# Rotary turn of the query and key heads: head by head on 32 partitions, or packed through DRAM onto 128 partitions

## The chip, the cores and the metric

The kernel runs on one core of a Trainium2 chip. TensorE (PE) multiplies, VectorE (DVE), ScalarE (ACT) and GpSimd (POOL) work element by element, SyncE (SP) issues most of the loads. The metric is the device time of one execution in microseconds (us), the median of several runs; lower is better.

## The reference

The kernel computes one decoder block for 512 tokens of width 1024. What concerns the change is the partial rotary embedding: of each of the 8 query heads and 2 key heads (width 128) the first 32 features are turned, 16 against 16; the other 96 stay as they are.

```python
def partial_rope(x, pos, rot_dim):          # rot_dim = 32 for q and k
    inv_freq = ROPE_THETA ** (-jnp.arange(0, rot_dim, 2, dtype=jnp.float32) / rot_dim)
    ang = pos.astype(jnp.float32)[..., None] * inv_freq
    ...
    xr = x[..., :rot_dim].astype(jnp.float32)
    x1, x2 = xr[..., : rot_dim // 2], xr[..., rot_dim // 2:]
    rot = jnp.concatenate([x1 * cos - x2 * sin, x2 * cos + x1 * sin], axis=-1)
    return jnp.concatenate([rot.astype(x.dtype), x[..., rot_dim:]], axis=-1)

# in the layer
q = partial_rope(q.reshape(bsz, s, N_HEADS, HEAD_DIM), positions, ROT_DIM)
k = partial_rope(k.reshape(bsz, s, N_KV_HEADS, HEAD_DIM), positions, ROT_DIM)
...
ki = layer_norm(ki, idx_k_ln_g, idx_k_ln_b)   # the indexer's key: normed, then turned by its own table
y_b = dsa_attention(q, k, v, qi, ki, wi)
```

## The kernel before, in words

**Layout.** Queries and keys are held transposed: features on the 128 partitions, the 512 tokens along a row. `qf[g]` holds heads 2g and 2g+1, `kf` the two key heads; each is `[128, 2, 512]` f32. The rows to be turned are partitions 0 to 31 of each.

**Every product is three.** Each f32 operand is split into a high part `hi` (ACT, a copy) and a rest `lo` (DVE, or POOL where the plan says so, a subtraction), and `mm3` (lines 107 to 109) issues hi by hi, hi by lo, lo by hi. Weights come in chunks: SP loads `raw`, ACT makes `hi` (line 163), DVE or POOL makes `lo` (line 167). `get(i, ahead=2)` prepares the chunk two further on before the current one is multiplied; there are three buffers each of `raw`, `hi` and `lo`.

**Order.** The schedule is written by hand: each engine executes its instructions in the order in which the code emits them, and waits by semaphores for the others. After the first projection (the key heads and query heads 0 to 3, until about 49 us) come eleven steps, counted by `qstep`: steps 0 and 1, then 2 and 3, are the two chunks each of `W_Q[0]` and `W_Q[1]` (the indexer's queries `qif`); 4, 5, 6 the three chunks of `vki` (values, the indexer's key, head weights); 7 and 8 `W_Q[2]`; 9 and 10 `W_Q[3]` (heads 4 to 7). At the start of step s `q_tasks` emits the list `QT[s]`, and only behind it the split of the chunk two further on. Then come eight chunks `W_AV` (the list `VT`).

**The key of the indexer.** In step 7 `ki_stats` takes mean and variance (DVE), and `rstd` on POOL (lines 430 and 431) makes the factor; `ki_norm` scales by it into `kin` on DVE (line 717). In the middle of step 8 `ki_T` has PE turn `kin` over (line 732, tile `kiT`), ACT and DVE bring it through `ki_a` and `ki_b`, and behind step 9 PE multiplies the result with the queries (lines 758 and 759, tile `idx`).

**POOL** has one queue: what it computes and the DMAs that it issues (`P.dma_start`) stand in one row, and a DMA that must wait for another to land holds up all behind it. In this stretch it issues the DMAs that lay out the tables `tab["q"]` and `tab["i"]` (lines 472 and 475), and then has little to do until `rstd`.

**The turn before.** For one head of 32 partitions `rope_a` shuffles the halves into `sh` (line 647), multiplies by the sine and by the cosine (648, 649), and `rope_b` adds (654): four DVE instructions, for ten heads, emitted in steps 0, 1, 2, 10 and with `W_AV`. `k_b` then splits the turned keys (`k_hi` on ACT, `k_lo` on DVE, line 435) in steps 7 and 8.

Of the kernel before, what the change touches and what calls it, by code (L numbers as in the profile page):

```python
# [9 lines left out]
F32 = mybir.dt.float32  # L10
# [48 lines left out]
def block_kernel(ctx: ExitStack, tc: tile.TileContext, x, x_t, w_in,  # L59
# [408 lines left out]
    def table_dma(kind, b):  # L468
        o = slice(b * 128, (b + 1) * 128)
        for h in range(2):  # L470
            if kind == "q":
                P.dma_start(tab["q"][h * 16:(h + 1) * 16, :, o], sn[b * 32:b * 32 + 16, 2 * h:2 * h + 2, :])
            else:
                for q in range(2):
                    P.dma_start(tab["i"][q * 64 + h * 8:q * 64 + h * 8 + 8, :, o],
                                sn[b * 32:b * 32 + 16:2, 2 * h:2 * h + 2, :])

    def run_chain(n):
        for _ in range(n):
# [116 lines left out]
    for kt in range(8):  # L596
        hi, lo = chunk[W1[kt]]
        V.tensor_sub(hT[kt][1], hfs[kt], f(hT[kt][0]))
        ensure(W1M[FIRST[kt]])
        if kt < 7:  # L600
            ensure(W1[kt + 1])
        wl = [(hi[:, 0, m * 128:(m + 1) * 128], lo[:, 0, m * 128:(m + 1) * 128]) for m in range(6)]
        hh, hl = hT[kt]
        kw = dict(skip_group_check=True)
        for m in range(6):
            T.matmul(outs[m], wl[m][0], hh, start=kt == 0, stop=False, **kw)
        for m in range(6):
            T.matmul(outs[m], wl[m][1], hh, start=False, stop=False, **kw)
        for m in range(6):
            T.matmul(outs[m], wl[m][0], hl, start=False, stop=kt == 7, **kw)  # L610
        if kt < 7:
            if kt < 5:
                low_w1(kt + 1)
            else:
                stream[W1[kt + 1]]["do"]()
            for k in (kt + 2,) if 0 < kt < 4 else (6, 7) if kt == 4 else ():
                row_scale(k)
            run_chain(kt == 1)
            ensure(W1M[BEHIND[kt]])
            stage_E(kt + 1)  # L620
        else:
            ensure(W_Q[0][1])
        if kt in (1, 2):
            A.activation(csb[:, (kt - 1) * 512:kt * 512], pc[:, (kt - 1) * 512:kt * 512], AF.Copy)
        if kt == 3:
            sines()
        if kt == 4:
            triu = mid.tile([128, 2, 128], F32, name="triu", tag="ql", bufs=2)[:, 0]
            SY.dma_start(triu, consts)
            for b in range(4):  # L630
                table_dma("q", b)
            for b in range(1, 4):
                table_dma("i", b)
            table_dma("i", 0)
    early.close()
    two.append(ctx.enter_context(tc.tile_pool(name="two", bufs=1, space=bass.MemoryType.PSUM)))
    for k in (6, 7):
        bank(k, "home")


    SW16 = [(p + 16) % 32 for p in range(32)]
    SW8 = [(p + 8) % 16 if p < 16 else p for p in range(32)]
    rp = {}

    def rope_a(key, v, kind, m, t0=0):
        sh = t512("sh")[:m, t0:]
        V.stream_shuffle(sh, v, SW16 if kind == "q" else SW8)
        V.tensor_mul(sh, sh, tab[kind][:m, 1, t0:])
        V.tensor_mul(v, v, tab[kind][:m, 0, t0:])
        rp[key] = (v, sh)  # L650
# [1 line left out]
    def rope_b(key):  # L652
        v, sh = rp[key]
        V.tensor_add(v, v, sh)


    kf = mid.tile([128, 2, S], F32, name="kf", tag="A0", bufs=1)
    qif = [mid.tile([128, 2, S], F32, name=f"qif{i}", tag=f"G{i}", bufs=1) for i in range(2)]
# [5 lines left out]
        A.activation(qf[m // 2][:, m % 2], pq[m], AF.Copy)  # L664
    for e in range(2):
        A.activation(kf[:, e], pk[e], AF.Copy)


    def qi_a(m):
# [14 lines left out]
    k_lo = mid.tile([128, 2, S], F32R, name="k_lo", tag="k_lo", bufs=1)  # L684

    k_pl = mid.tile([128, 2, 128], F32, name="k_pl")

    def k_a(h):
        rope_a(("k", h), kf[:32, h], "q", 32)

    def k_b(h):
        split(k_hi[:, h], k_lo[:, h], kf[:, h])
# [155 lines left out]
            iu[0] += 1  # L848
            n -= 1

    def q_rope(m):
        rope_a(("q", m), qf[m // 2][:32, m % 2], "q", 32)

    qstep = [0, 0]
    QT = {0: [lambda: q_rope(0), lambda: k_a(0)],
          1: [lambda: k_a(1), lambda: rope_b(("q", 0)), lambda: rope_b(("k", 0))],
          2: [lambda: rope_b(("k", 1)), lambda: qi_a(0)],
          3: [lambda: qi_b(0, 1), lambda: qi_a(1), lambda: qi_b(0, 0)],
          4: [lambda: qi_b(1, 1), lambda: qi_a(2), lambda: qi_b(1, 0)],
          5: [lambda: qi_b(2, 1), lambda: qi_a(3), lambda: qi_b(2, 0)],  # L860
          6: [lambda: qi_b(3, 1), lambda: qi_b(3, 0)],
          7: [ki_stats, lambda: k_b(0), ki_norm],
          8: [lambda: k_b(1)],
          10: [lambda: q_rope(1)]}

    def q_tasks():
        s = qstep[0]
# [39 lines left out]
        opt_b(W_Q[g], 8, hT, ((6, 7), (0, 1), (0, 1), (2, 3))[g], q_evac(g), q_tasks, q_post, q_mid, t0=0 if g > 1 else 128)  # L907


    vg = [mid.tile([128, 2, D], F32, name=f"vg{i}", tag=f"P{i}", bufs=1) for i in range(2)]  # L910
    lng = mid.tile([128, D], F32, name="lng", tag="G0", bufs=1)
    lnb = mid.tile([128, D], F32, name="lnb", tag="G1", bufs=1)
# [11 lines left out]
    def ws_mask():  # L924
        late["wmT"] = mid.tile([128, 8, 128], F32, name="wmT", tag="G2", bufs=1)
        V.tensor_tensor(late["wmT"], ws, triu[:, None, :].to_broadcast([128, 8, 128]), op=OP.mult)

    VT = {0: [lambda: q_rope(2), lambda: rope_b(("q", 1))],
          1: [lambda: q_rope(3), lambda: rope_b(("q", 2))],
          2: [lambda: q_rope(4), lambda: rope_b(("q", 3))],  # L930
          3: [lambda: q_rope(5), lambda: rope_b(("q", 4))],
          4: [lambda: q_rope(6), lambda: rope_b(("q", 5))],
          5: [lambda: q_rope(7), lambda: rope_b(("q", 6))],
          6: [lambda: rope_b(("q", 7)), load_bs], 7: [ws_mask]}
    for _ in range(16):
        bg.append((1.4, topk_max))
        bg.append((1.4, topk_replace))
# [1147 lines left out]
```

## Time and profile before

| | before |
|---|---|
| median of 3 runs | 784.74 us (784.25 to 785.29) |
| span of the profiled execution, first to last instruction | 783.3 us |
| mean granted TensorE clock | 0.993 |
| busy share PE, DVE, ACT, POOL | 99%, 85%, 55%, 23% |
| POOL's DMA queue (software dynamic) | 9232 packets, 30.15 MB, 15.2% of 16 engines' span |

The profiled execution's own time is its span and what lies around it; the median of the runs is 1.4 us above the span. An instruction's duration can overlap the next one on its engine, on PE above all: there the distance from start to start counts. A row of the timeline gives start, duration, engine, line, what is written from what, and in brackets how long the engine was idle before and what ended that.

### The profile page before, as it was taken

The page shows a single profiled execution, that of the slowest core. Times are in us where ns is not written, and L with a number is a line of the kernel's source. Part 1 is how long each engine was busy: PE and PEld are TensorE (multiplying, and loading weights), DVE is VectorE, ACT ScalarE, POOL GpSimd, SP SyncE. Part 2 cuts the span into 40 slices and gives each one's busy share as a digit, 9 for nine tenths or more (in the row PEclk, how much of TensorE's full clock was granted, in tenths as well). Part 3 has the DMA queues.
Part 4 walks back from the last instruction along what each step waited for, and adds up shares of the span by engine and source line. Part 5 has one row for each costly group of instructions (what it writes and reads, how often), then busy time and mean ns, then how long its engine had stood idle before and what let it go on. Part 6 is the DMA issues. An engine that isn't in the chain of part 4 may idle for free.

```text
span 783.3 us, 12307 instructions
## 1 busy us (share of the span) xinstructions
PE 774.1 (99%) x4579; PEld 688.5 (88%) x4579; DVE 666.6 (85%) x1128; ACT 427.3 (55%) x757; POOL 179.0 (23%) x234
## 2 busy tenths in 40 slices
PE   8999999999999999999999999999999999999996
PEld 7899888888888888988888899999999999888885
DVE  7989788887889559986697879989999888998877
ACT  6664445423332246666546577655566666676654
POOL 4870222312344412100020000313132223000001
PEclk8999999999999999999999999999999999999999
DMA  9953252332435558627682603879897967556762
GB/s 345 416 187 125 82 168 75 135 99 89 132 123 206 210 188 225 180 75 265 220 248 33 209 1 109 253 231 300 268 254 230 270 205 210 162 187 206 219 216 112
DMA packets 51277, 146.24 MB, mean 187 GB/s; under 512 B 13969, under 2 KB 14737, under 8 KB 51218
## 3 DMA queue, kind: packets, MB, share of 16 engines
q1 hardware_dynamic: 41408, 114.35, 42.2%
q0 software_dynamic: 9232, 30.15, 15.2%
q10 hardware_dynamic: 578, 0.95, 0.3%
q8 instruction: 36, 0.59, 0.3%
q14 instruction: 23, 0.19, 0.1%
HBM read 140.97 MB, written 27.27 MB: 215 GB/s over the span
## 4 chain that ended last, share of the span: by engine, by line
PE 81%; DVE 9%; DMA 6%; ACT 2%; issue 1%; SPq 0%; POOL 0%; POOLq 0%; DVEq 0%; ACTq 0%
PE R L107 8%; PE R L109 8%; PE R L108 8%; PE pb L108 5%; PE pb L109 5%; PE pb L107 5%; PE pfo L109 4%; PE pfo L107 4%; PE pfo L108 4%; DMA mraw<-in_w_shsc_dram 4%; DVE mraw L255 2%; PE pav L109 2%; PE pav L108 2%; PE pav L107 2%; PE po L109 2%; PE po L107 2%
## 5 line engine op out<-in xcount | busy, mean ns | idle before, releaser
L163 ACT ACTIVATE hi<-raw 128x1024 fp32r<-128x1024 f32 (+4 forms) x106 | 107.4, 1014 | 94.4 <-PE pb L108 38.9
L167 DVE TENSOR_TENSOR lo<-raw,hi 128x1024 fp32r<-128x1024 f32 (+2 forms) x73 | 85.4, 1171 | 24.0 <-ACT hi L163 23.6
L167 POOL TENSOR_TENSOR lo<-raw,hi 128x1024 fp32r<-128x1024 f32 x25 | 59.9, 2398 | 106.7 <-ACT hi L163 101.2
L107 PE MATMUL pb<-h,hi 128*128 128x512 f32 (+1 forms) x192 | 73.6, 383 | 0.0
L108 PE MATMUL pb<-h,hi 128*128 128x512 f32 (+1 forms) x192 | 73.0, 380 | 0.0
L109 PE MATMUL pb<-h,lo 128*128 128x512 f32 (+1 forms) x192 | 73.0, 380 | 0.0
L108 PE MATMUL pfo<-lo,za 128*128 128x512 f32 (+1 forms) x144 | 55.2, 383 | 0.0
L109 PE MATMUL pfo<-hi,za 128*128 128x512 f32 (+1 forms) x144 | 55.2, 383 | 0.0
L107 PE MATMUL pfo<-hi,za 128*128 128x512 f32 (+1 forms) x144 | 55.2, 383 | 0.0
L255 DVE CUSTOM_DVE_ANT_0 mraw<-mraw,csb,cols 128x1024 f32<-128x1024 f32 x27 | 39.3, 1455 | 18.6 <-DMA mraw<-in_w_shsc_dram 18.6
L389 POOL COPY sm<-sm 128x1 f32<-128x1 f32 x36 | 25.0, 696 | 92.3 <-ACT sm L388 92.2
L107 PE MATMUL R<-tb,hi 128*128 128x256 f32 x160 | 44.2, 276 | 0.0
L108 PE MATMUL R<-tb,hi 128*128 128x256 f32 x160 | 44.2, 276 | 0.0
L109 PE MATMUL R<-tb,lo 128*128 128x256 f32 x160 | 44.2, 276 | 0.0
L107 PE MATMUL R<-tb,sx 128*128 128x256 f32 x160 | 44.2, 276 | 0.0
L108 PE MATMUL R<-tb,sx 128*128 128x256 f32 x160 | 44.2, 276 | 0.0
L109 PE MATMUL R<-tb,sx 128*128 128x256 f32 x160 | 44.2, 276 | 0.0
L109 PEld LDWEIGHTS pb<-h,lo 128*128 128x128 f32 x192 | 36.0, 188 | 6.3
L108 PEld LDWEIGHTS pb<-h,hi 128*128 128x128 f32 x192 | 36.1, 188 | 6.0
L107 PEld LDWEIGHTS pb<-h,hi 128*128 128x128 f32 x192 | 36.1, 188 | 6.0
L369 POOL DMA_DIRECT2D wsum<-in_w_ffn_out_dram x24 | 19.6, 822 | 72.3 <-DMA wsum<-wsum 39.7
L108 PEld LDWEIGHTS pfo<-lo,za 128*128 128x128 f32 x144 | 27.1, 188 | 5.4
(395 smaller groups left out, 2563.2 us busy)
## 6 DMA issues: line engine op xcount, KB each, us to landing
raw<-in_w_ffn_in_dram SPq DMA_DIRECT2D x44, 512.0 KB
raw<-in_w_in_dram SPq DMA_DIRECT2D x40, 512.0 KB
wsum<-in_w_ffn_out_dram POOLq DMA_DIRECT2D x30, 512.0 KB, 7.5
mraw<-in_w_shsc_dram SPq DMA_DIRECT2D x27, 512.0 KB
raw<-wsum SPq DMA_DIRECT2D x20, 512.0 KB
s<-in_w_shsc_dram SPq DMA_DIRECT2D x14, 512.0 KB
raw<-in_w_ffn_out_dram SPq DMA_DIRECT2D x13, 512.0 KB
wsum<-wsum POOLq DMA_DIRECT2D x10, 512.0 KB, 5.9
```

Of the source, the lines that this page charges most:

```text
L107: T.matmul(o, wh, rh, start=start, stop=False, **kw)
L108: T.matmul(o, wh, rlo, start=False, stop=False, **kw)
L109: T.matmul(o, wlo, rh, start=False, stop=stop, **kw)
L163: A.activation(hi[:, :m], e["raw"][:, :m], AF.Copy)
L167: e["lo"].tensor_sub(lo[:, :m], e["raw"][:, :m], f(hi[:, :m]))
L255: V.tensor_tensor_reduce(out=raw[:, c], in0=raw[:, c], in1=(csb if s > 1 else pc)[:, c], scale=scale, scalar=sums.pop(0), op0=OP.mult, op1 ...
L369: P.dma_start(wsum_at(n, c), src, max_dma_last_dim=4096, accum_op=OP.add)
L389: P.tensor_copy(t, t)
```

## The change

Ten turns of one head become three turns of a packed tile. A pack holds four query heads (`q0` heads 0 to 3, `q4` heads 4 to 7) or the two key heads twice (`k`). `load` writes the rows to be turned to DRAM, 16 partitions to a DMA, and reads them back into one tile of 128 partitions (`a`), and once more with the halves exchanged (`b`), in place of the shuffle. `turn` is two products and a sum on 128 partitions. `back` writes the result to DRAM and reads the rows into `qf` and `kf` again. The sine table is laid out on 128 partitions by four more DMAs (`table_spread`). All these DMAs are POOL's. The loads of `q0` and `k` stand right behind the first projection, the turn of `k` at the end of `QT[5]`, that of `q0` at the end of `QT[6]`; `q4` is loaded behind step 10 and turned at `VT[4]`.

```diff
--- before.py
+++ after.py
@@ -469,11 +469,16 @@
         o = slice(b * 128, (b + 1) * 128)
         for h in range(2):
             if kind == "q":
-                P.dma_start(tab["q"][h * 16:(h + 1) * 16, :, o], sn[b * 32:b * 32 + 16, 2 * h:2 * h + 2, :])
+                P.dma_start(tab["q"][h * 64:h * 64 + 16, :, o], sn[b * 32:b * 32 + 16, 2 * h:2 * h + 2, :])
             else:
                 for q in range(2):
                     P.dma_start(tab["i"][q * 64 + h * 8:q * 64 + h * 8 + 8, :, o],
                                 sn[b * 32:b * 32 + 16:2, 2 * h:2 * h + 2, :])
+
+    def table_spread():
+        for n in (16, 32):
+            for h in range(2):
+                P.dma_start(tab["q"][h * 64 + n:h * 64 + 2 * n], tab["q"][h * 64:h * 64 + n])
 
     def run_chain(n):
         for _ in range(n):
@@ -632,19 +637,19 @@
             for b in range(1, 4):
                 table_dma("i", b)
             table_dma("i", 0)
+            table_spread()
     early.close()
     two.append(ctx.enter_context(tc.tile_pool(name="two", bufs=1, space=bass.MemoryType.PSUM)))
     for k in (6, 7):
         bank(k, "home")
 
 
-    SW16 = [(p + 16) % 32 for p in range(32)]
     SW8 = [(p + 8) % 16 if p < 16 else p for p in range(32)]
     rp = {}
 
     def rope_a(key, v, kind, m, t0=0):
         sh = t512("sh")[:m, t0:]
-        V.stream_shuffle(sh, v, SW16 if kind == "q" else SW8)
+        V.stream_shuffle(sh, v, SW8)
         V.tensor_mul(sh, sh, tab[kind][:m, 1, t0:])
         V.tensor_mul(v, v, tab[kind][:m, 0, t0:])
         rp[key] = (v, sh)
@@ -653,6 +658,38 @@
         v, sh = rp[key]
         V.tensor_add(v, v, sh)
 
+
+    class Packed:
+
+        def __init__(self, tag, srcs):
+            ne = 2 * len(srcs)
+            self.srcs, self.ne = srcs, ne
+            self.d = [dram.tile([128, S], F32, name=f"pk{tag}{k}") for k in range(2)]
+            t = at_line(base, tag, (2, S), F32, "pk")
+            self.a, self.b = t[:, 0], t[:, 1]
+
+        def load(self):
+            ne, rows = self.ne, 16 * self.ne
+            d = self.d[0][:2 * rows].rearrange("(h e p) n -> h p e n", h=2, p=16)
+            for j, t in enumerate(self.srcs):
+                for h in range(2):
+                    P.dma_start(d[h, :, 2 * j:2 * j + 2], t[16 * h:16 * h + 16])
+            for o, flip in ((self.a, 0), (self.b, 1)):
+                for h in range(2):
+                    for r in range(0, 64, rows):
+                        P.dma_start(o[64 * h + r:64 * h + r + rows], self.d[0][rows * (h ^ flip):rows * (h ^ flip) + rows])
+
+        def turn(self):
+            V.tensor_mul(self.b, self.b, tab["q"][:, 1])
+            V.tensor_mul(self.a, self.a, tab["q"][:, 0])
+            V.tensor_add(self.a, self.a, self.b)
+
+        def back(self):
+            P.dma_start(self.d[1], self.a)
+            d = self.d[1].rearrange("(h e p) n -> h p e n", h=2, p=16)
+            for j, t in enumerate(self.srcs):
+                for h in range(2):
+                    P.dma_start(t[16 * h:16 * h + 16], d[h, :, 2 * j:2 * j + 2])
 
     kf = mid.tile([128, 2, S], F32, name="kf", tag="A0", bufs=1)
     qif = [mid.tile([128, 2, S], F32, name=f"qif{i}", tag=f"G{i}", bufs=1) for i in range(2)]
@@ -664,6 +701,9 @@
         A.activation(qf[m // 2][:, m % 2], pq[m], AF.Copy)
     for e in range(2):
         A.activation(kf[:, e], pk[e], AF.Copy)
+    packs = {"q0": Packed("S2_4", qf[:2]), "k": Packed("S2_5", [kf])}
+    for n in ("q0", "k"):
+        packs[n].load()
 
 
     def qi_a(m):
@@ -684,9 +724,6 @@
     k_lo = mid.tile([128, 2, S], F32R, name="k_lo", tag="k_lo", bufs=1)
 
     k_pl = mid.tile([128, 2, 128], F32, name="k_pl")
-
-    def k_a(h):
-        rope_a(("k", h), kf[:32, h], "q", 32)
 
     def k_b(h):
         split(k_hi[:, h], k_lo[:, h], kf[:, h])
@@ -848,20 +885,18 @@
             iu[0] += 1
             n -= 1
 
-    def q_rope(m):
-        rope_a(("q", m), qf[m // 2][:32, m % 2], "q", 32)
+    def rope_pack(n):
+        packs[n].turn()
+        packs[n].back()
 
     qstep = [0, 0]
-    QT = {0: [lambda: q_rope(0), lambda: k_a(0)],
-          1: [lambda: k_a(1), lambda: rope_b(("q", 0)), lambda: rope_b(("k", 0))],
-          2: [lambda: rope_b(("k", 1)), lambda: qi_a(0)],
+    QT = {2: [lambda: qi_a(0)],
           3: [lambda: qi_b(0, 1), lambda: qi_a(1), lambda: qi_b(0, 0)],
           4: [lambda: qi_b(1, 1), lambda: qi_a(2), lambda: qi_b(1, 0)],
-          5: [lambda: qi_b(2, 1), lambda: qi_a(3), lambda: qi_b(2, 0)],
-          6: [lambda: qi_b(3, 1), lambda: qi_b(3, 0)],
+          5: [lambda: qi_b(2, 1), lambda: qi_a(3), lambda: qi_b(2, 0), lambda: rope_pack("k")],
+          6: [lambda: qi_b(3, 1), lambda: qi_b(3, 0), lambda: rope_pack("q0")],
           7: [ki_stats, lambda: k_b(0), ki_norm],
-          8: [lambda: k_b(1)],
-          10: [lambda: q_rope(1)]}
+          8: [lambda: k_b(1)]}
 
     def q_tasks():
         s = qstep[0]
@@ -907,6 +942,8 @@
         opt_b(W_Q[g], 8, hT, ((6, 7), (0, 1), (0, 1), (2, 3))[g], q_evac(g), q_tasks, q_post, q_mid, t0=0 if g > 1 else 128)
 
 
+    packs["q4"] = Packed("S2_6", qf[2:])
+    packs["q4"].load()
     vg = [mid.tile([128, 2, D], F32, name=f"vg{i}", tag=f"P{i}", bufs=1) for i in range(2)]
     lng = mid.tile([128, D], F32, name="lng", tag="G0", bufs=1)
     lnb = mid.tile([128, D], F32, name="lnb", tag="G1", bufs=1)
@@ -925,13 +962,7 @@
         late["wmT"] = mid.tile([128, 8, 128], F32, name="wmT", tag="G2", bufs=1)
         V.tensor_tensor(late["wmT"], ws, triu[:, None, :].to_broadcast([128, 8, 128]), op=OP.mult)
 
-    VT = {0: [lambda: q_rope(2), lambda: rope_b(("q", 1))],
-          1: [lambda: q_rope(3), lambda: rope_b(("q", 2))],
-          2: [lambda: q_rope(4), lambda: rope_b(("q", 3))],
-          3: [lambda: q_rope(5), lambda: rope_b(("q", 4))],
-          4: [lambda: q_rope(6), lambda: rope_b(("q", 5))],
-          5: [lambda: q_rope(7), lambda: rope_b(("q", 6))],
-          6: [lambda: rope_b(("q", 7)), load_bs], 7: [ws_mask]}
+    VT = {4: [lambda: rope_pack("q4")], 6: [load_bs], 7: [ws_mask]}
     for _ in range(16):
         bg.append((1.4, topk_max))
         bg.append((1.4, topk_replace))
```

On POOL the stretch between the laying out of the tables and `rstd`, loads first (`pkS_40` and `pkS_50` are the DRAM buffers of `q0` and `k`, `pk` the packed tiles):

```order
 L475 DMA tab_i<-sn 8x2x128 x16
-L791 MEMSET sco_629 128x128
-L775 AFFINE_SELECT sco_629<-sco_629 128x128
+L481 DMA tab_q<-tab_q 16x1024 x2
+L481 DMA tab_q<-tab_q 32x1024 x2
+L676 DMA pkS_40_621<-qf_611 16x2x512 x2
+L676 DMA pkS_40_621<-qf_612 16x2x512 x2
+L680 DMA pk<-pkS_40_621 64x512 x4
+L676 DMA pkS_50_624<-kf 16x2x512 x2
+L680 DMA pk<-pkS_50_624 32x512 x8
```

Twenty-two DMAs now follow the last table DMA. Behind them in the same row, up to `rstd` (the last two lines), come the ways back (`pkS_51` for `k`, `pkS_41` for `q0`):

```order
+L828 MEMSET sco_657 128x128
+L812 AFFINE_SELECT sco_657<-sco_657 128x128
+L688 DMA pkS_51_625<-pk 128x512
+L692 DMA kf<-pkS_51_625 16x2x512 x2
+L688 DMA pkS_41_622<-pk 128x512
+L692 DMA qf_611<-pkS_41_622 16x2x512 x2
+L692 DMA qf_612<-pkS_41_622 16x2x512 x2
 L430 TENSOR_SCALAR sm<-mv 128x4
 L431 TENSOR_TENSOR sm<-sm,mhalf 128x4
```

Where only a memset and a select stood ahead of `rstd`, eight DMAs of two ways back stand there now. On DVE, from the end of step 5's indexer work to the first statistics of step 7, before:

```order
L681 TENSOR_TENSOR qil_606<-qif_602,qil_606 64x384
L167 TENSOR_TENSOR lo<-raw,hi 128x1024
L654 TENSOR_TENSOR qif_602<-qif_602,sh 128x384
L680 TENSOR_TENSOR qih_604<-qif_602,qih_604 64x384
L681 TENSOR_TENSOR qil_606<-qif_602,qil_606 64x384
L167 TENSOR_TENSOR lo<-raw,hi 128x1024
L708 BN_STATS bst<-kit 128x6
```

And the same place now:

```order
L683 TENSOR_TENSOR pk<-pk,tab_q 128x512
L684 TENSOR_TENSOR pk<-pk,tab_q 128x512
L685 TENSOR_TENSOR pk<-pk 128x512
L167 TENSOR_TENSOR lo<-raw,hi 128x1024
L659 TENSOR_TENSOR qif_606<-qif_606,sh 128x384
L720 TENSOR_TENSOR qih_608<-qif_606,qih_608 64x384
L721 TENSOR_TENSOR qil_610<-qif_606,qil_610 64x384
L683 TENSOR_TENSOR pk<-pk,tab_q 128x512
L684 TENSOR_TENSOR pk<-pk,tab_q 128x512
L685 TENSOR_TENSOR pk<-pk 128x512
L167 TENSOR_TENSOR lo<-raw,hi 128x1024
L745 BN_STATS bst<-kit 128x6
```

The turn of `k` stands ahead of the split of step 7's chunk, that of `q0` ahead of the split of step 8's chunk; the twelve instructions of three heads that stood in steps 0 to 2 are gone from DVE.

## Rows read from the trace of the kernel before

**Rows 1.** Busy time by stretch: engine, instructions in brackets; granted clock, DMA share, GB/s.

```profile
65.60:79.90 14.30, 14.30 (x97) 14.30 (x97) 12.69 (x27) 7.23 (x14) 0.00 (x0) 1.00 0.33 113
79.90:104.90 25.00, 25.00 (x114) 20.68 (x113) 19.93 (x35) 12.75 (x28) 5.78 (x7) 1.00 0.44 142
```

**Rows 2.** Timeline of PE: start, duration, engine, line, out<-in.

```profile
79.91 0.39 PE L107 MATMUL pb<-h,hi 128*128 128x512 f32 x1
...
85.37 0.39 PE L107 MATMUL pb<-h,hi 128*128 128x512 f32 x1
...
88.10 0.60 PE L732 MATMUL kiT<-ident,kin 128*128 128x128 f32 x4
88.45 0.47 PE L107 MATMUL pb<-h,hi 128*128 128x512 f32 x1
...
96.74 0.39 PE L758 MATMUL idx<-ki_t,qih 128*128 128x512 f32 x1
96.97 0.39 PE L759 MATMUL idx<-ki_t,qih 128*128 128x512 f32 x1
```

**Rows 3.** Timeline of DVE, steps 5 to 9 and the end of W_AV.

```profile
73.61 1.23 DVE L167 TENSOR_TENSOR lo<-raw,hi 128x1024 fp32r<-128x1024 f32 x1
...
76.48 0.55 DVE L681 TENSOR_TENSOR qil<-qif,qil 64x384 fp32r<-64x384 f32 x1
...
82.87 1.11 DVE L717 TENSOR_SCALAR kin<-kit,mv,sm 128x128 f32<-128x128 f32 x4
83.90 1.41 DVE L721 TENSOR_TENSOR v_lo<-pv,v_hi 128x256 fp32r<-128x256 f32 x4
...
89.62 0.74 DVE L647 STREAM_SHUFFLE sh<-kr 128x512 f32<-128x512 f32 x1
...
93.11 0.69 DVE L435 TENSOR_TENSOR ki_t<-kr,ki_t 128x512 fp32r<-128x512 f32 x1 [0.70 <-ACT ki_t L434]
...
143.46 1.66 DVE L769 SCALAR_TENSOR_TENSOR sco<-rl,wi,sco 128x256 f32<-128x256 f32 x3 [1.25 <-ACT rl L766]
```

**Rows 4.** Groups on DVE by shape, 45 to 145 us: busy us, mean ns.

```profile
L648 DVE TENSOR_TENSOR sh<-sh,tab_q 32x512 f32<-32x512 f32 x10 | 11.6, 1156 | 0.3
L649 DVE TENSOR_TENSOR qf<-qf,tab_q 32x512 f32<-32x512 f32 x8 | 7.6, 954 | 0.0
...
L647 DVE STREAM_SHUFFLE sh<-qf 32x512 f32<-32x512 f32 x8 | 5.8, 723 | 0.0
L654 DVE TENSOR_TENSOR qf<-qf,sh 32x512 f32<-32x512 f32 x8 | 5.4, 672 | 0.0
```

**Rows 5.** Timeline of POOL from the tables to `rstd`.

```profile
45.33 7.27 POOL L475 DMA_DIRECT2D tab_i<-sn  x13
52.75 1.67 POOL L475 DMA_DIRECT2D tab_i<-sn  x3 [0.16 <-issue]
...
80.91 0.19 POOL L430 TENSOR_SCALAR sm<-mv 128x4 f32<-128x4 f32 x1 [25.90 <-DVE mv L709]
81.18 1.05 POOL L431 TENSOR_TENSOR sm<-sm,mhalf 128x4 f32<-128x4 f32 x1
```

**Rows 6.** POOL's DMAs at 45:50, 50:55, 294:321, 351:365: count, KB, median to landing.

```profile
tab_i<-sn POOLq DMA_DIRECT2D x9, 8.0 KB, 3.9
...
tab_i<-sn POOLq DMA_DIRECT2D x8, 8.0 KB, 2.3
...
ld<-pd POOLq DMA_DIRECT2D x16, 128.0 KB, 4.3
...
xr<-in_x_dram POOLq DMA_DIRECT2D x4, 512.0 KB, 4.9
```

**Rows 7.** Timeline at 294:300, SP's queue and POOL: rows through DRAM `pd`.

```profile
294.22 2.73 SPq L1145 DMA_DIRECT2D pd<-tn  x4
...
299.36 2.06 POOL L1151 DMA_DIRECT2D ld<-pd  x4 [20.10 <-DMA pd<-tn]
```

**Rows 8.** The chain that ended last, shares of the span by engine (page, part 4).

```profile
PE 81%; DVE 9%; DMA 6%; ACT 2%; issue 1%; SPq 0%; POOL 0%; POOLq 0%; DVEq 0%; ACTq 0%
```

## The prediction

> **What bounds the kernel now.** I read the stretches first. From the first projection's end to the end of step 10 PE is busy for the whole of each stretch, at a granted clock of 1.00, while DVE runs at 80 to 90% and POOL hardly works [rows 1]. A busy PE need not be at its peak, so I look at the timeline of PE next: two products of 512 columns start 0.23 us apart, at 96.74 and 96.97 [rows 2], and the whole of step 7, 24 products, takes 5.46 us from 79.91 to 85.37, which is 0.23 each. There is no gap in it. PE is the bound here, and whatever DVE saves is worth nothing unless PE waits for it. A wait that reaches PE, on the other hand, is lost in full, since the rest of the program is PE's too.
>
> So I don't ask what the change saves but which instruction of PE now gets its data later than it needs it. The nearest is the turning over of `kin`: PE does it at 88.10 and goes on at 88.45 [rows 2], in the middle of step 8. `kin` stood ready at 83.98 (82.87 and 1.11) [rows 3], 4.1 us early. It waits for `rstd` on POOL, which took 1.32 us, from 80.91 to 82.23, and had been idle for 25.90 us before [rows 5]. That idle row of POOL is where the change puts its DMAs.
>
> **DVE.** The ten heads cost 11.6 us in the sine products of all ten, 7.6, 5.8 and 5.4 in the other three kinds of the eight query heads [rows 4], and some 4.1 in those of the two key heads (two times 0.72 + 0.67 + 0.67): 34.5 us. A DVE instruction on 128 partitions and 512 columns takes 0.69 (at 93.11) [rows 3], no longer than one on 32 partitions, so nine of them cost 6.2. DVE gets 28 us back. On PE's time this is worth 0, by what was said above; the work that hides it is PE's own.
>
> **POOL's way to the turn of `k`.** The last table DMA is issued by 54.42 (52.75 and 1.67), and 16 of them took from 45.33 to there, 0.57 each [rows 5]. Behind it stand 22 DMAs of 64 or 128 KB. Where one reads what another wrote, POOL waits for the landing, and all behind it waits too. Call a landing of 64 KB, counted from its issue, L. The second pair of the sine table waits for the first (L). The fourth DMA from there is issued 2.3 later; the loads of `q0` wait for the writes of `q0` (L), four of them are issued (2.3); then come the writes of `k`, whose loads wait for them (L); the last of the eight loads is issued 4.0 after the first and lands after L. In all the packed `k` is there at 54.4 + 2.3 + 2.3 + 4.0 + 4 L = 63.0 + 4 L.
>
> No row shows a 64 KB landing here. From below: 8 KB at a quiet time, 2.3; from above: 128 KB in a busy one, 4.3 [rows 6]. A straight line from 8 KB to the 512 KB of `xr` at 4.9 gives 2.6 for 64 KB and 3.6 for 256 KB, an estimate. For a write to DRAM the fourth `pd` starts about 296.3 and POOL, which waited for it, goes on at 299.36: 3.1 for 128 KB [rows 7]. I take L = 2.9 and 3.8 for 256 KB, somewhat above the line, since weight loads pass at the same time (DMA share 0.33 to 0.44) [rows 1] and the 8 KB ones took 3.9 at a busier time [rows 6]. So `k` is there at 74.6. DVE comes to its turn by 73.6, where the split of step 7's chunk stood [rows 3], or up to a microsecond earlier with less to do. It waits a microsecond or two. Behind the turn stands that split: 74.6 + 1.9 + 1.2 = 77.7, and PE wants it in the third product of step 7, at 80.4. This is covered, with 2.7 to spare.
>
> **From the turn to `kin`.** The turn of `k` takes 1.9 (0.61 + 0.61 + 0.69; instructions overlap a little). From the split to the end of the indexer's work that follows it takes 3.4 (73.61 to 77.03) [rows 3], and then comes the turn of `q0`, 1.9: done at 74.6 + 7.2 = 81.8. The split of step 8's chunk behind it is done at 83.0, wanted at 85.8. On POOL the way back of `k` is through by then (76.5 + 3.8 + 1.1 = 81.4). The 256 KB of `q0` are written (3.8), POOL waits for the landing, issues four reads (2.3), and only then comes `rstd` (1.3); then `kin` (1.1). Sum: 81.8 + 3.8 + 2.3 + 1.3 + 1.1 = 90.3. PE's last part of the turning over starts about 88.4. **PE waits 1.9 us**, some tenths more for the handing over between engines, which I haven't counted: 2.0. In general the wait is the time of `k`'s landing, plus that of the 256 KB write, less 76.5.
>
> **Nothing more behind it?** From `kin` DVE needs 1.3 for `v_lo`, two splits and a `k_lo` (2.9), and 4.2 from the shuffle to the end of the indexer key's rest (89.62 to 93.80) [rows 3]: 8.4. PE needs 8.9 from the turning over to the product that reads it (88.10 to 96.97) [rows 2]. This fits, by 0.5. ACT's split of `k` waits for its rows until about 84, before anybody needs it. `q4` holds POOL for about 3.8 + 2.3 = 6.1 after its turn, and a chunk is split two ahead, that is two times 5.5 us: hidden; without that cover it would cost up to those 6.1.
>
> The sum against the profiled execution: 783.3 + 2.0 = 785.3 of span; the median of the runs is 1.4 above the span, so 784.74 + 2.0 = **786.7 us**, 0.25% more. About 0.2%, or 1.6 us, is what a measurement of this kernel can tell from no change; the forecast is only just beyond it.
>
> **The rivals.** *Hidden.* If landings are short, the wait vanishes: with L = 2.3 the packed `k` is there at 72.2, the turn begins when DVE is there, at 72.6 to 73.6, and with 3.1 for the write the formula gives 0.2 or less. Up to 1.6 us of wait this case counts as no change: 784.7 to 786.3. For it speaks the 2.3 of the nearest row in time [rows 6]; against it that this is for 8 KB and that each of the four landings would have to be like it. The Trainium skill, in DMA: Bandwidth & Descriptors, section Anatomy of one DMA — SWDGE (gpsimd) path, fits such a DMA as 2.0 us and its bytes at 436 GB/s; by that estimate 64 KB take 2.15 and 256 KB 2.6, the wait would be gone and the time 784.7. By that rule the 8 KB rows should read 2.0, and the trace shows 2.3 to 3.9, so I give it no more weight than the rows do.
>
> *Long.* If weight loads in flight stretch each landing to 3.6 and the write to 4.6, then `k` is there at 77.4 and the wait is 5.5: 790.2; with 3.9, the busier row, `k` is there at 78.6, the split of step 7's chunk comes 1.3 late as well, and 792 is in reach. For it: `ld` at 4.3 [rows 6]; against it the DMA share of 0.33 to 0.44 here, with 142 GB/s at most, and that `ld` came four at a time.
>
> *Faster.* DVE has 9% of the chain that ended last [rows 8]. If that came from work which DVE carries over from here, 28 us less of it would bring it forward, but PE idles only 1% of the span, some 8 us, most of them at its two ends; if a quarter were DVE's doing, it would give 2: 782.7. It decides if DVE is still behind when `W_AV` ends. At 143.46 it sat idle 1.25 us for ACT [rows 3], so it has nothing to carry over. That the turn is not packed after all, or undone elsewhere, I see no way to.
>
> **How the numbers follow.** A wait between 1.6 and 4.2 us: 0.42, with its own range 786.3 to 789. Hidden: 0.37. Long: 0.16. Faster: 0.05. The range of 784.2 to 790.8 reaches over hidden and into long; about 0.07 lie above, 0.06 below. Slower by over 0.2%: 0.42 + 0.16 = 0.58; within: 0.37; faster: 0.05.
>
> **What would show it.** In the changed kernel: POOL idle before the loads that wait; DVE idle for a DMA ahead of the turn of `k`, for 1 to 2 us; `rstd` starting about 87.9 instead of 80.91, right behind the last read of `q0`; PE idle ahead of `kiT` by some 2 us, and nowhere else; DVE's busy time some 28 us less and its idle time as much more. If `rstd` comes before 86 and PE shows no gap, landings were shorter than 2.9; if PE also waits ahead of step 7 or 8, they were longer. I'm wrong in kind if PE waits for `idx`, or for a chunk in `W_AV`, or if the time falls.

## The result, and the profile after

| | before | after |
|---|---|---|
| median | 785.0 us (784.25 to 785.29, 4 runs) | 789.41 us (788.75 to 790.79, 4 runs) |
| span of the profiled execution | 783.3 us | 787.0 us |
| POOL's DMA queue | 9232 packets, 30.15 MB | 10912 packets, 34.22 MB |

The changed kernel takes 1.0058 times as long, with an interval of 1.0044 to 1.0073: 4.4 us more, where 2.0 were forecast. First the page's busy times of the changed kernel, then its list of waits (engine and line, what it waited for; us in total, times, longest).

```profile
PE 775.1 (98%) x4579; PEld 688.6 (87%) x4579; DVE 642.2 (82%) x1087; ACT 426.5 (54%) x757; POOL 200.6 (25%) x277
```

```profile
PE kiT L769 <- DVE kin L754: 3.0, 1, 3.0
...
PE pb L109 <- DVE lo L167: 0.2, 1, 0.2
```

DVE does less and PE waits more. Of the waits of PE that were not there before, two lie in the stretch of the change: a large one ahead of `kiT`, at the predicted place, and a small one in step 7, where none was predicted. PE's timeline shows both, and something more.

```profile
79.14 0.40 PE L108 MATMUL pb<-h,hi 128*128 128x512 f32 x1
79.73 0.50 PE L109 MATMUL pb<-h,lo 128*128 128x512 f32 x1 [0.19 <-DVE lo L167]
...
87.35 0.39 PE L109 MATMUL pb<-h,lo 128*128 128x512 f32 x1
90.70 1.24 PE L769 MATMUL kiT<-ident,kin 128*128 128x128 f32 x4 [2.97 <-DVE kin L754]
91.60 0.77 PE L107 MATMUL pb<-h,hi 128*128 128x512 f32 x1
92.17 0.63 PE L108 MATMUL pb<-h,hi 128*128 128x512 f32 x1
...
93.88 0.41 PE L109 MATMUL pb<-h,lo 128*128 128x512 f32 x1
```

From start to start: in step 7 the third product comes 0.59 after the second instead of 0.23, and the next (80.07) 0.34 after that: 0.47 lost. Ahead of `kiT` PE stands for 2.97 (3.12 from start to start: 87.35 to 90.70, less 0.23), and the four parts of the turning over take 0.90 (90.70 to 91.60) where they took 0.35 before [rows 2], since each waits for its part of `kin`, which DVE makes in four (through SyncE's queue, below, they take 0.85 at a full clock too): 0.55 more. And then the products of 512 columns stand 0.57 and 0.42 apart, not 0.23. The stretches show why (the third figure from the right is the granted clock, the one behind it the DMA share).

```profile
87.00:90.00 3.00, 0.74 (x4) 0.27 (x2) 0.00 (x0) 0.77 (x1) 2.84 (x6) 1.00 0.61 209
90.00:91.00 1.00, 0.30 (x2) 0.23 (x2) 0.70 (x3) 0.00 (x0) 0.26 (x1) 0.75 0.00 0
91.00:92.00 1.00, 1.00 (x5) 0.85 (x5) 1.00 (x5) 0.00 (x0) 0.00 (x0) 0.50 0.00 0
...
93.00:94.00 1.00, 1.00 (x4) 0.78 (x3) 1.00 (x2) 0.00 (x0) 0.00 (x0) 0.54 0.00 0
94.00:95.00 1.00, 1.00 (x6) 0.83 (x5) 1.00 (x2) 0.00 (x0) 0.00 (x0) 1.00 0.00 0
```

PE is idle from about 87.6 to 90.7; in 90 to 91 the clock falls, and until about 93.9 it is at 0.50, the lower level of 1.2 GHz. The five products from 91.60 to 93.88 take 2.28 instead of 5 times 0.23, so 1.1 are lost. Together: 0.47 + 3.12 + 0.55 + 1.1 = 5.2 us of PE's time between 79 and 94, against no gap there before. In this execution PE was 1.0 ahead when step 7 began (78.91; before 79.91 [rows 2]), through its start-up. Its last product starts 4.2 later than before (780.25 against 776.05): 1.0 and 4.2 are the 5.2, so nothing was lost anywhere else. The span grew by 3.8, since the few us behind PE's last product were 0.4 shorter; the medians differ by 4.4.

How late things are on the way to `kin` shows on POOL and then on DVE:

```profile
58.02 0.50 POOL L481 DMA_DIRECT2D tab_q<-tab_q  x1 [2.69 <-DMA tab_q<-tab_q]
...
59.67 2.02 POOL L676 DMA_DIRECT2D pkS<-qf  x4
65.29 2.09 POOL L680 DMA_DIRECT2D pk<-pkS  x4 [3.60 <-DMA pkS<-qf]
67.37 1.04 POOL L676 DMA_DIRECT2D pkS<-kf  x2
70.24 1.01 POOL L680 DMA_DIRECT2D pk<-pkS  x2 [1.83 <-DMA pkS<-kf]
71.82 2.94 POOL L680 DMA_DIRECT2D pk<-pkS  x6 [0.57 <-DMA pkS<-kf]
...
84.18 0.59 POOL L688 DMA_DIRECT2D pkS<-pk  x1 [1.61 <-DVE pk L685]
86.86 2.01 POOL L692 DMA_DIRECT2D qf<-pkS  x4 [2.09 <-DMA pkS<-pk]
88.95 0.19 POOL L430 TENSOR_SCALAR sm<-mv 128x4 f32<-128x4 f32 x1
```

```profile
71.14 0.56 DVE L721 TENSOR_TENSOR qil<-qif,qil 64x384 fp32r<-64x384 f32 x1
76.52 0.69 DVE L683 TENSOR_TENSOR pk<-pk,tab_q 128x512 f32<-128x512 f32 x1 [4.82 <-DMA pk<-pkS]
...
78.46 1.22 DVE L167 TENSOR_TENSOR lo<-raw,hi 128x1024 fp32r<-128x1024 f32 x1
...
83.19 0.69 DVE L685 TENSOR_TENSOR pk<-pk 128x512 f32<-128x512 f32 x1
...
90.30 1.11 DVE L754 TENSOR_SCALAR kin<-kit,mv,sm 128x128 f32<-128x128 f32 x4 [3.32 <-POOL sm L431]
```

POOL stops at each load for the write before it, as the order said. DVE stands still for 4.82 ahead of the turn of `k`, and for 3.32 ahead of `kin`, because `rstd` stands behind `q0`'s way back. The landings (count, KB each, median us from issue), of 54 to 76 and of 76 to 90:

```profile
pk<-pkS POOLq DMA_DIRECT2D x8, 64.0 KB, 2.1
...
pkS<-qf POOLq DMA_DIRECT2D x4, 64.0 KB, 4.2
tab_q<-tab_q POOLq DMA_DIRECT2D x2, 64.0 KB, 3.7
pkS<-kf POOLq DMA_DIRECT2D x2, 64.0 KB, 2.9
...
pkS<-pk POOLq DMA_DIRECT2D x2, 256.0 KB, 2.4
```

### The profile page after: what moved, and what is told of

Same layout as the page of the kernel before. It is cut to its first block, busy times and chain, and to the rows that moved or that the text cites. A ratio compares the mean times of both kernels' runs of the same rounds, so it can differ in the third digit from the quotient of the medians.

```text
span 787.0 us, 12340 instructions
## 1 busy us (share of the span) xinstructions
PE 775.1 (98%) x4579; PEld 688.6 (87%) x4579; DVE 642.2 (82%) x1087; ACT 426.5 (54%) x757; POOL 200.6 (25%) x277
## 3 DMA queue, kind: packets, MB, share of 16 engines
q0 software_dynamic: 10912, 34.22, 16.9%
## 4 chain that ended last, share of the span: by engine, by line
PE 71%; DVE 10%; DMA 4%; ACT 2%; issue 1%; POOLq 0%; POOL 0%; DVEq 0%
PE R L108 8%; PE R L109 8%; PE R L107 8%; DMA mraw<-in_w_shsc_dram 4%; PE pfo L108 4%; PE pfo L107 4%; PE pfo L109 4%; PE pb L108 4%; PE pb L107 4%; PE pb L109 4%; DVE mraw L255 2%; PE pav L108 2%; PE pav L107 2%; PE pav L109 2%; PE po L109 2%; PE po L108 2%
## 5 line engine op out<-in xcount | busy, mean ns | idle before, releaser
L389 POOL COPY sm<-sm 128x1 f32<-128x1 f32 x36 | 23.3, 648 | 84.1 <-ACT sm L388 83.9
L806 DVE SCALAR_TENSOR_TENSOR sco<-rl,wi,sco 128x512 f32<-128x512 f32 (+2 forms) x24 | 19.4, 809 | 22.6 <-ACT rl L803 12.7
```

Of the source, the lines that this page charges most:

```text
L389: P.tensor_copy(t, t)
L806: V.scalar_tensor_tensor(sco[i], rl[:, :n], wi[:, i, h:h + 1], sco[i], op0=OP.mult, op1=OP.add)
```

## The experiments

Each was timed in five rounds against the kernel before on the same chip. Which of these things costs how much is what they are to tell: the lateness of `k` on DVE, the place of `rstd` behind the way back on POOL, the DMAs' mere traffic, the clock, or less work on DVE.

**The way back of `q0` behind `rstd`.**

```diff
-          6: [..., lambda: rope_pack("q0")],
-          7: [ki_stats, lambda: k_b(0), ki_norm],
+          6: [..., lambda: packs["q0"].turn()],
+          7: [ki_stats, lambda: packs["q0"].back(), lambda: k_b(0), ki_norm],
```

> The changed kernel, but POOL issues the way back of q0 behind rstd instead of ahead of it; nothing else moves. Theory (POOL's row of waiting DMAs makes rstd late): rstd starts when the variance is there, about 86.4 instead of 88.95, kin ends near 88.9, PE waits about 1.1 us ahead of kiT instead of 3.0, the granted clock stays at 1.00 behind it, and the 0.4 us ahead of step 7's third product stays: 786.2 to 787.0. Rival (the 4 MB of extra DMA traffic slows what PE needs, wherever POOL's row stands): as the changed kernel, 789. Rival (DVE's wait for the packed k alone is the cause): PE's wait ahead of kiT stays near 3 us.

785.6 us, 1.0012 (1.0003 to 1.0020), somewhat better than the 786.2 to 787.0 that I had expected. Its wait and POOL's row of `rstd`:

```profile
PE kiT L769 <- DVE kin L754: 0.8, 1, 0.8
```

```profile
87.66 0.58 POOL L430 TENSOR_SCALAR sm<-mv 128x4 f32<-128x4 f32 x1 [3.88 <-DVE mv L746]
```

POOL now waits for the statistics, not DVE for POOL. The wait falls from 3.0 to 0.8, the clock stays at 1.00, and some four fifths of the loss are gone with one exchange in POOL's row. What is left is DVE's own lateness. (The profiled execution is the longest of the twelve, 787.98; it loses another 1.2 us far behind this stretch, from 250 us on, which I leave open.)

**Everything later.** `k` is turned in step 8, `q0` in step 9, behind the indexer's key; the DMAs are the same.

```diff
-          5: [..., lambda: rope_pack("k")],
-          6: [..., lambda: rope_pack("q0")],
-          7: [ki_stats, lambda: k_b(0), ki_norm],
-          8: [lambda: k_b(1)]}
+          5: [...],
+          6: [...],
+          7: [ki_stats, ki_norm],
+          8: [lambda: rope_pack("k")],
+          9: [lambda: rope_pack("q0")],
+          10: [lambda: k_b(0), lambda: k_b(1)]}
```

> The changed kernel with the turns of k and q0 moved behind the indexer's key: k at the start of step 8, q0 at step 9, the split of the keys at step 10. The same DMAs and the same DVE work. Theory: nobody that PE waits for stands behind a landing any more, PE shows no gap from 49 to 160 us, and the time is that of the kernel before, 784.5 to 785.7. Rival (traffic or POOL's work as such): 788 to 789. Rival (DVE's 28 us are worth something once the wait is gone): below 784.

784.79 us, 1.0002 (0.9993 to 1.0010); PE waits nowhere between 50 and 110 us. Its DMA queue moves the same 34.22 MB, `q4` included, so the traffic by itself costs PE nothing that shows, 0.1% at most. And with all the cost gone, the kernel is equal to the one before and not faster.

**No turn at all.** The kernel before, with the turning of the ten heads left out (a part of the computation that is missing here).

```diff
-    QT = {0: [lambda: q_rope(0), lambda: k_a(0)],
-          1: [lambda: k_a(1), lambda: rope_b(("q", 0)), lambda: rope_b(("k", 0))],
-          2: [lambda: rope_b(("k", 1)), lambda: qi_a(0)],
+    QT = {2: [lambda: qi_a(0)],
...
-    VT = {0: [lambda: q_rope(2), lambda: rope_b(("q", 1))],
...
+    VT = {6: [load_bs], 7: [ws_mask]}
```

> The kernel before without any turn of the query and key heads (this part of the computation is left out; the tables are still made): DVE has 34.5 us less to do and no DMA is added. Theory: PE is the bound in this stretch, so the time is that of the kernel before, 784.5 to 785.5. Rival (DVE's load in this stretch reaches PE later): 782 to 783.5.

784.16 us, 0.9995 (0.9986 to 1.0003). All that the turn costs on DVE is worth 0 to 1 us at most. Its page:

```profile
PE 774.8 (99%) x4579; PEld 689.6 (88%) x4579; DVE 635.9 (81%) x1078; ACT 426.6 (54%) x757; POOL 175.2 (22%) x234
```

Without the turn DVE is busy for 635.9, before 666.6: the ten heads took 30.7 of busy time, not the 34.5 that I had summed up from means, in which overlapping instructions count twice. With the nine new ones of 0.7 it is 642.2, the changed kernel's number.

**Keeping PE at work in the wait.** The changed kernel with small products of the identity (128 columns) on PE ahead of `kiT`, into a bank that nothing reads; 20 in one kernel, 12 in the other.

```diff
+            w = bank(7, "warm2")
+            for _ in range(20):
+                T.matmul(w[:, :128], ident, ident, start=True, stop=True)
```

> The changed kernel with 20 small products of the identity on PE ahead of kiT, into a PSUM bank that is free: they take some 2.2 us and fall into PE's wait of 3.0. Theory (the wait also costs a spell of low granted clock, 90 to 94 us, about 1.5 us): the clock stays at 1.00 behind kiT and the time falls by about 1.5, to 787.5 to 788.3. Rival (the low clock costs nothing, the loss is the wait alone): unchanged, 789.4, or more by what the small products overrun.

> As e4_kept_warm with 12 small products instead of 20: the 20 took 4.5 us, longer than the wait that they should fill, and overran it by about 1.3. Twelve take 2.7. Theory (the spell of low clock costs about 1.5 us): 1.4 to 1.8 us less than the changed kernel, a ratio of about 1.0035 to 1.0042 to the kernel before, clock 1.00 throughout. Rival (the low clock costs nothing): ratio 1.0055 or more.

With 20: 788.49 us, 1.0047 (1.0035 to 1.0059), a little above what I had expected. They took 4.46, from 87.07 to 91.53, while `kin`, begun at 89.33, was done at 90.45, so they made a wait of about 1.3 themselves (the product behind the turning over starts 2.56 after `kin` is begun, in the changed kernel 1.30). With 12: 787.35 us, 1.0031 (1.0019 to 1.0043), a little below. The stretch that was at half clock, with 12:

```profile
91.00:92.00 1.00, 1.00 (x5) 0.69 (x6) 1.00 (x5) 0.20 (x1) 0.00 (x0) 1.00 0.00 0
```

The granted clock is 1.00 there, and `kin` as late as before. Against the changed kernel 0.0027 of the time, 2 us, come back, with an uncertainty of about 1.5; the rows of the low spell gave 1.1. That the clock is a cost of its own, behind the wait, is shown. That it is nearer 1 us the rows show too: in the profiled execution with 12 PE began step 7 at 79.79, only 0.1 ahead of the kernel before, showed no gap in step 7 and started the product behind the turning over at 91.46 (changed kernel 91.60). From step 7 on it lost 3.1 there, against 5.2, and of these 2.1 the smaller lead is 0.9, the clock 1.1.

**The table earlier.** The four DMAs of the sine table between those of the indexer's table, where POOL should not have to wait for them.

```diff
-            for b in range(1, 4):
-                table_dma("i", b)
+            table_dma("i", 1)
+            table_dma("i", 2)
+            table_spread(16)
+            table_dma("i", 3)
             table_dma("i", 0)
-            table_spread()
+            table_spread(32)
```

> The changed kernel with the four DMAs that spread the sine table issued between the table DMAs (after the second and the fourth block of the indexer's table) instead of behind them: POOL doesn't stop for the landing of the first pair, which took 3.2 us of its row; everything else stays. Theory (landings in POOL's row reach PE one for one): the packed k is there about 3 us earlier, PE's wait ahead of kiT falls from 3.0 to 0 to 0.5, that ahead of step 7 and the low clock go: 784.5 to 785.4. Rival (PE's wait is set by the way back of q0 alone): wait unchanged near 3 us, 788 to 789.5.

786.44 us, 1.0023 (1.0013 to 1.0033): a miss. I had expected the wait at `kiT` to be gone; it was 2.5. POOL's rows (line numbers are one higher here):

```profile
54.45 2.77 POOL L475 DMA_DIRECT2D tab_i<-sn  x5 [0.96 <-DMA tab_i<-sn]
...
58.24 2.02 POOL L677 DMA_DIRECT2D pkS<-qf  x4
64.14 2.09 POOL L681 DMA_DIRECT2D pk<-pkS  x4 [3.88 <-DVE lo L167]
```

POOL now stopped among the indexer's tables instead, and the first write of `q0` left 1.4 earlier (58.24 for 59.67). Even so its load still had to wait (the 3.88 are put down to DVE, which the load doesn't need; it is the landing of `pkS`). The landings of the first two of these writes and of the last two (windows 58.2 to 59.2 and 59.3 to 60.2):

```profile
pkS<-qf POOLq DMA_DIRECT2D x2, 64.0 KB, 2.2
```

```profile
pkS<-qf POOLq DMA_DIRECT2D x2, 64.0 KB, 4.1
```

What sets the last two (59.26 and 59.76) apart is a load of 512 KB of weights that SyncE issued right beside them, at 59.42. In the changed kernel it stood 0.4 ahead of the first write, and the four took 4.2 in the median:

```profile
59.42 0.33 SPq L145 DMA_DIRECT2D raw<-in_w_in_dram  x1
```

```profile
59.25 0.33 SPq L145 DMA_DIRECT2D raw<-in_w_in_dram  x1
```

In all the kernels here the first writes of `q0` or `k` show this: sixteen that were issued within 1.1 us behind such a load took 3.2 to 4.7, and seven that had none in the 3.5 us ahead of them and none in the 0.3 us behind took 2.2 to 2.4; the others lie between, 2.4 to 4.3.

So 3.3 of waiting (2.69 and 0.61) turned into 2.46 at another place (0.96 there and 1.50 at 52.35), and of what was won 0.95 reached the turn of `k` (75.58 for 76.52) and `kin` (89.35 for 90.30). But after 2.5 idle the clock stayed at 1.00, which saves the 1.1 of the changed kernel: with the earlier `kin` that makes 2.1, and PE's rows show it (the product behind the turning over starts at 90.60 instead of 91.60, at the same lead of 1.0). The ratios differ by 0.0035, 2.7 us, uncertain by 1.4. Step 7 had no gap here, and this saved nothing: PE came to `kiT` that much sooner and stood there, since `kin` sets when it goes on.

**One pack alone.** `k` packed, the query heads not turned; then the queries packed, `k` not turned (each leaves out a part of the computation).

```diff
-    for n in ("q0", "k"):
+    for n in ("k",):
```

> The changed kernel with only the key heads packed and turned; the query heads aren't turned at all (that part of the computation is left out). Theory (only the sum of the two packs is too long): without q0's loads k is there about 69, DVE doesn't wait for it, no way back of q0 stands ahead of rstd; no gap on PE, 784.2 to 785.2. Rival (the keys' way through DRAM is what PE waits for): 786 or more.

> The changed kernel with only the query heads packed and turned, in both packs; the key heads aren't turned (that part is left out). Theory: q0 is there before DVE gets to it, its turn ends about 78 to 79, the way back holds POOL until about 83.5, rstd ends near 85 and kin near 86.3, under the 4.1 us that kin had to spare: no gap on PE, 784.3 to 785.3. Rival (q0's way back ahead of rstd is enough by itself): PE waits ahead of kiT, 786 or more.

`k` alone: 784.77 us, 1.0000 (0.9992 to 1.0008), turned at 71.98, `rstd` at 80.49. The queries alone: 785.46 us, 1.0006 (0.9998 to 1.0015), `rstd` at 83.64. Neither waits at `kiT`. Either way through DRAM is hidden; only the two in one row are too long.

**`k` first.** The loads of `k` ahead of those of `q0`.

```diff
-    for n in ("q0", "k"):
+    for n in ("k", "q0"):
```

> The loads of k stand ahead of those of q0, nothing else is changed. Theory (k's packed rows come late because they stand behind two waits for q0, and with them DVE, the turn of q0 and rstd): POOL issues the eight reads of k from about 63.5 on, k is there at 70, DVE doesn't wait ahead of its turn, the turn of q0 ends 3 us earlier (about 81 instead of 83.88), kin stands ready by 88 instead of 91.4, and PE waits 0 to 0.5 ahead of kiT, with the clock at 1.00: 784.5 to 785.5, 1.000 to 1.001 of the kernel before. Rival (the way back of q0, not k's landing, holds rstd; or q0's rows now come as late as k's did): DVE waits ahead of the turn of q0 instead, and PE waits 1.5 or more: 786.5 or more.

786.33 us, 1.0018 (1.0004 to 1.0032), and its runs lie far apart, from 784.22 to 789.43; the profiled one is of the long ones, 788.57. The time lies above the 784.5 to 785.5 expected, and near the rival's. Half of the theory holds there: `k` was early and DVE was through with `q0` 5 us earlier than in the changed kernel (78.12 for 83.19 in the last row of the turn). Yet `rstd` came only 0.9 earlier.

```profile
78.12 0.69 DVE L685 TENSOR_TENSOR pk<-pk 128x512 f32<-128x512 f32 x1
```

```profile
79.79 1.04 POOL L692 DMA_DIRECT2D kf<-pkS  x2 [4.04 <-DMA pkS<-pk]
80.82 0.59 POOL L688 DMA_DIRECT2D pkS<-pk  x1
85.98 2.00 POOL L692 DMA_DIRECT2D qf<-pkS  x4 [4.57 <-DMA pkS<-pk]
88.06 0.19 POOL L430 TENSOR_SCALAR sm<-mv 128x4 f32<-128x4 f32 x1
```

Both writes of 256 KB made POOL wait for 4.04 and 4.57, where the changed kernel's waits were 2.13 and 2.09. The DMA views of 75 to 80 and of 80 to 87:

```profile
pkS<-pk POOLq DMA_DIRECT2D x1, 256.0 KB, 4.3
...
pkS<-pk POOLq DMA_DIRECT2D x1, 256.0 KB, 4.9
```

Against 2.4 in the changed kernel. What differs is the weight load of 512 KB beside each write. SyncE's row of the load at the second write, with `k` first and then in the changed kernel:

```profile
79.97 0.33 SPq L145 DMA_DIRECT2D raw<-in_w_in_dram  x1
```

```profile
85.05 0.33 SPq L145 DMA_DIRECT2D raw<-in_w_in_dram  x1
```

With `k` first the loads are issued 0.6 and 0.8 ahead of the writes (74.59 and 75.17, 79.97 and 80.82), in the changed kernel 0.9 behind them (78.84 and 79.70, 84.18 and 85.05). A write behind a load lands 2 us later, and a microsecond decides which of the two comes first. The last kernel below has the same order of instructions up to this write and shows the other case: PE began step 7 1.4 later there (80.01 for 78.58), the load was issued 1.4 later (76.02 for 74.59), the write at the same time (75.16 for 75.17), and it landed in 2.4 instead of 4.3:

```profile
76.02 0.33 SPq L145 DMA_DIRECT2D raw<-in_w_in_dram  x1
```

```profile
pkS<-pk POOLq DMA_DIRECT2D x1, 256.0 KB, 2.4
```

That this is why the runs with `k` first lie so far apart fits, but only one of them was profiled.

**Through SyncE's queue.** The packs' DMAs issued by SyncE; the table's stay on POOL.

```diff
-                    P.dma_start(d[h, :, 2 * j:2 * j + 2], t[16 * h:16 * h + 16])
+                    SY.dma_start(d[h, :, 2 * j:2 * j + 2], t[16 * h:16 * h + 16])
```

> The packs' DMAs (writes, reads, ways back) are issued by SyncE instead of POOL; the table's four stay with POOL. Theory (rstd is late only because it stands behind these DMAs on POOL): rstd runs right behind mv, kin is early, no wait ahead of kiT: 784.5 to 785.7, if the weight loads that now stand behind SyncE's waits are early enough. Rival (a waiting queue costs whoever stands behind it, here the chunks of weights): loads of raw come late, PE waits for hi or lo in steps 1 to 9, several us: 788 or more, slower than the changed kernel.

786.69 us, 1.0018 (1.0010 to 1.0027), between the two. Between 50 and 90 us ACT and DVE wait like this:

```profile
ACT hi L163 <- DMA raw<-in_w_in_dram: 5.4, 1, 5.4
...
DVE lo L167 <- ACT hi L163: 9.1, 3, 4.8
```

SyncE stood at its own waits, the loads of weights behind them came late, ACT split late, and DVE came to the turn of `k` at 76.91 without waiting for a DMA: as late as in the changed kernel, for another reason. `rstd` came at 86.84, right behind its statistics, and PE waited 0.7 at `kiT`, the clock staying at 1.00. The price of a waiting queue went to those behind it, as the rival said, though it was smaller than its 788.

**`k` first and the way back behind `rstd`**: the two edits above together.

> Two edits together: the loads of k ahead of those of q0, and the way back of q0 behind rstd. Theory (rstd was late by two things in a row: DVE, which waited for k, and POOL, which stood in q0's way back; with k first and alone, two write landings of 4.0 and 4.6 us beside a weight load ate most of what DVE had won): rstd runs right behind the statistics, unless k's own way back, which still stands ahead of it, lands after 82; then kin is ready by 86.5, no wait of PE in steps 7 and 8, and the time is the kernel's before: 784.3 to 785.4, 1.000 to 1.0008, in all runs alike. Rival (something else in the change, such as its traffic or q4's way back, costs a microsecond as well): 785.5 to 786.5 with no gap ahead of kiT, or a gap there of 0.7 as with the way back alone moved.

784.48 us, 1.0000 (0.9991 to 1.0009), all runs between 783.86 and 785.74. `rstd` and the turning over:

```profile
82.82 0.58 POOL L430 TENSOR_SCALAR sm<-mv 128x4 f32<-128x4 f32 x1 [3.92 <-DVE mv L746]
```

```profile
88.20 0.60 PE L769 MATMUL kiT<-ident,kin 128*128 128x128 f32 x4
```

No wait of PE is left in the stretch. Two exchanged positions give back the whole 4.4 us; the packed turn with all its DMAs, `q4`'s too, then costs what the old one did. No version here beats the kernel before, and with no turn at all (0.9995) there is hardly anything to win.

## Why the prediction was right, point by point

**The sign and the place** were right. PE is the bound, DVE's savings are worth nothing (no turn at all: 0.9995), and the loss is a wait ahead of `kiT` that comes through POOL's row of DMAs and `rstd` (way back moved: 3.0 falls to 0.8). The time lies in the range, 2.7 above the forecast. It is just above the 786.3 to 789 of the case that I held likeliest, and in the range only because that reaches into *long*. These are the terms that were mis-sized.

**The landing L of 64 KB: too short for one of the four.** `k` was there at 76.5, 1.9 later in all: the write of `q0` took 2.7 more than in the sum, the rest 0.8 less. The table was laid out by 59.6, as the sum had it. From the first write of `q0` (59.67) to the first load behind it (65.29) 5.6 passed, where the sum had one L of 2.9. It left out that the four writes are issued one behind the other, the fourth 1.5 after the first, and it took too little for their landing, 4.2. The other terms were right or too long: the writes of `k` held POOL for 2.9 and once more for 0.57, and the reads of `k` landed in 2.1. I had raised L a little for weight loads that pass at a DMA share of 0.33 to 0.44 [rows 1]. A mean share says nothing of the order, and by all the writes here it was the order that counted: the write of `q0` stood right behind a load (59.25), and writes of the same size with no load near them took 2.2 to 2.4 (see under the table earlier).

The Trainium skill, DMA: Bandwidth & Descriptors, section Anatomy of one DMA — SWDGE (gpsimd) path, gives 2.0 us and the bytes at 436 GB/s, an estimate of 2.15 for 64 KB and 2.6 for 256 KB. The trace agrees where no load is ahead (256 KB in 2.4; the reads of 64 KB in 2.1, writes in 2.2 to 2.4) and not beside other traffic (64 KB in 2.9 to 4.2, 256 KB in 4.3 and 4.9).

**The split of step 7's chunk: cover of 2.7 used up.** It was done at 79.68 and not at 77.7, 2.0 late, and PE was 1.0 ahead of its former time: 3.0 against 2.7. PE lost 0.47. "Nowhere else" was wrong by this. It cost no time, since PE then stood ahead of `kiT` for that much less.

**From the turn to `kin`.** From the turn of `k` to the end of that of `q0` it took 7.36 (predicted 7.2); the write of 256 KB, to the next issue, 2.7 (3.8); the four reads 2.1 (2.3); `rstd` and `kin` as predicted; and 0.3 pass between the turn and the write. Sum: 1.9 + 0.2 - 1.1 - 0.2 + 0.3 = 1.1, and `kin` was done at 91.4 instead of 90.3. The write was cheaper because it was ahead of the weight load; with `k` first the same write, behind one, took 4.9. This order was not foreseen, so the 1.1 that it took off the lateness is luck.

**The wait.** The 2.0 forecast were counted to the last part of the turning over. To these come the 1.1, and 0.5 because PE was that much ahead (1.0 less the 0.47 of step 7): 3.6. Measured: 3.12 of wait and 0.55 in the turning over, 3.7.

**The clock: missing in the sum.** After this wait PE ran at half clock for some 3 us, which cost 1.1 by the rows, and 2, uncertain by 1.5, by the times (clock held at 1.00 with 12 small products). The prediction had looked at the clock only to say that it was at 1.00. Forecast were 2.0, and PE's last product came 4.2 later: of the 2.2 between them the later `kin` is 1.1 and the clock 1.1. The 1.0 by which PE was ahead made the wait of this execution longer, and not by itself its time. But a shorter wait, 2.5 with the table earlier, left the clock at 1.00, so the lead may have had a part in its fall; only one execution of the changed kernel was profiled.

**The signs named ahead.** DVE stood for 4.8 ahead of the turn of `k` and not for 1 to 2: `k` came 1.9 later, and DVE, with less to do, was there at 71.7 instead of 73.6 [rows 3], where I had allowed a microsecond. PE's gap in step 7 is the sign that was named for landings longer than 2.9. `rstd` began at 88.95 (87.9). DVE's busy time fell by 24.4 (28), for the reason shown with no turn at all.

**What was held for hidden** was: PE shows no wait for `idx`, in `W_AV` or for `q4`; the kernels with late turns and with queries alone say the same.

**The rivals.** *Hidden* asked for landings of 2.3; the last reads had that, the writes ahead of them did not. *Long* named the right thing, weight loads that stretch the landings, but it was so for the write of `q0` alone (4.2) and not for each; its write of 4.6 didn't come, and the time near its 790.2 came by the clock. *Faster* is out: neither 24.4 nor 30.7 us less work on DVE moved the end.

## What to carry to other kernels

An engine that issues DMAs which wait for each other is blocked for all that stands behind them in its row: put the short instruction that the bound engine needs (here `rstd`, 1.3 us) ahead of them, and among the waiting chains the one needed first. Where the engine that gets relief is not the bound, the work moved elsewhere can at best cost nothing; cost its waits, not its bytes, count the issue of several DMAs in a row (0.5 us each here) as well as the landing of the last, and price a landing by what is issued right ahead of it, not by a mean DMA share. A wait of the bound engine can cost more than its length, if the clock falls behind it.

## What the runs showed of the hardware that I had not expected

- After 2.97 us idle (changed kernel) and 2.88 (`k` first) PE's granted clock fell to 0.50 for some 3 us, although PE was at work again; after 2.5 (table earlier) and 0.7 to 0.8 it stayed at 1.00. Small products that write to an unread bank kept it at 1.00.
- A write of 256 KB to DRAM took 2.4 us to land with a weight load of 512 KB issued behind it and 4.3 and 4.9 with one issued ahead of it; the difference of 2 us in one landing is as large as the whole wait that was forecast. A write of 64 KB took 2.2 to 2.4 us with no such load in the 3.5 us ahead of it and the 0.3 us behind it (seven writes in four kernels), and 3.2 to 4.7 when issued within 1.1 us behind one (sixteen in nine).
